# A two-layer decoder trunk: the last layer ends with the tokens on the partitions instead of the channels

## The chip, the cores and the metric

The kernel runs on 1 core of one Trainium2 chip. The metric is the device time of one execution in microseconds (us); lower is better.

## What is computed

256 tokens of 1024 channels (f32) pass through two layers. Each layer has a mixer and then a PEER expert retrieval; the text below is about the end of the second layer's PEER and the final norm:

```python
def block(x_t):                                   # 128 tokens
    ...
    u = u_emb[eidx]; v = v_emb[eidx]              # experts of 128 x 128 product keys
    act = gelu(einsum('thkd,td->thk', u, x_t))
    return einsum('thk,thkd->td', gate * act, v)
...
x = x + g2 * peer(h, ...)                         # g2: one gate per channel, from c
return rmsnorm(x, final_norm)                     # over the 1024 channels of a token
```

The kernel does PEER densely: for each of the 128 first keys it multiplies all tokens with a 1024 x 128 slice of the first table (`u_emb`), keeps gated activations in `ga`/`gb`, and then multiplies these with the slices of the second table (`v_emb`).

## The kernel before, in words

**Layout.** x lies in SBUF as `xt`, 128 partitions of 8 channel chunks x 256 tokens, so that channels are on the partitions: a gate or a norm weight is a scalar per partition, and a sum over channels goes through TensorE with a column of ones.

**Second table, lines 1136 to 1158.** A loop over 126 of the 128 slices. In round i, `csplit(i + 2)` splits one row of the activations into a high part `ch` (ScalarE, L1095) and a rest `cl` (VectorE, L1096). `take()` hands out the slice i and prepares the one two rounds ahead: `hi` on ScalarE (L194), `lo` on VectorE (L201), from `raw`, which SyncE's queue loads from HBM 512 KB at a time (L169), several rounds ahead, each load waiting for a buffer that `lo` frees. Then 12 products of 128x512 (three of hi/lo with ch/cl, for 2 token halves t and 2 channel halves) accumulate in four banks `acc[2 * t + half]` (token rows x 512 channels). Buffers of `ch`, `cl`, `hi` and `lo` are three deep, so the work for round i + 2 waits for the products of round i - 1. The order on each engine is the order in which the code issues.

`xt` is used as scratch during PEER; it is stored to HBM (`x_dram`) before and read back on ScalarE's DMA queue in round 118 (L1148).

**End, lines 1160 to 1221.** The last two slices go bank by bank (6 products each, in the order half, t). Each bank is copied to SBUF (`y`, L1184 to L1187), turned back with 128x128 transposes on TensorE (L1171), multiplied by the gate and added to `xt` (L1175), squared on ScalarE (L367). Squares are added in part on VectorE (L355), and their sum over channels is taken by 1-column products with ones (L377). `rstd` takes root and reciprocal (L384, L385), spreads it over the partitions by a product (L387, L390), and 8 products of x, weight and rstd on VectorE (L1219) give the output, stored in four pieces of 256 KB (L1221) from the queues of SyncE and ScalarE by turns.

Of the kernel before, what the change touches and what calls it, by code (L numbers as in the profile page):

```python
# [10 lines left out]
F32 = mybir.dt.float32  # L11
# [5 lines left out]
AF = mybir.ActivationFunctionType  # L17
OP = mybir.AluOpType
AX = mybir.AxisListType

P = 128
D = 1024
S = 256
NCH = 8
EPS = 1e-6
HEADS = 8
NKEYS = 128
# [10 lines left out]
V_ADAB, V_NMIX, V_NFFN, V_FIN, V_GV, V_PS, V_GS, V_C, NV = 0, 96, 112, 128, 136, 140, 144, 145, 153  # L38
# [8 lines left out]
def trunk(ctx, tc, xT, crow, vecs, consts_in, pos, lamv, bs, cnt, ws, wpool, ada, ev_in, ev_out,  # L47
          od_in, od_out, wq, sk, u_emb, v_emb, out):
    nc = tc.nc
# [7 lines left out]
    dram = ctx.enter_context(tc.tile_pool(name="dram", bufs=1, space=bass.MemoryType.DRAM))  # L57
    ctx.enter_context(tc.manual_schedule())

    dma = nc.sync.dma_start  # L60
# [4 lines left out]
    def aux():  # L65
        return aux_ps.tile([P, 512], F32, name="aux")


    xt = const.tile([P, NCH, S], F32, name="xt")
    vec = const.tile([P, NV], F32, name="vec")  # L70
    cst = const.tile([P, NK], F32, name="cst")
    c_dram = dram.tile([1, D], F32, name="c_dram")
    ident = const.tile([P, P], F32, name="ident")
    iota = const.tile([P, P], F32, name="iota")
    ones = const.tile([P, P], F32, name="ones")
    epst = const.tile([P, 1], F32, name="epst")
# [7 lines left out]
    iotah = const.tile([P, P], F16, name="iotah")  # L84
    nc.vector.tensor_copy(iotah, iota)
    x_dram = dram.tile([P, NCH * S], F32, name="x_dram")
    tabs = const.tile([P, 2, TOPK], F16, name="tabs")
    nc.vector.memset(epst, EPS)
    mod = [const.tile([P, 48], F32, name=f"mod{l}") for l in range(2)]
# [5 lines left out]
    acc = []  # L95
# [48 lines left out]
    def opened(name, **kw):  # L144

        es = ExitStack()
        return es.enter_context(tc.tile_pool(name=name, bufs=1, **kw)), es.close
# [4 lines left out]
    def open_extra(l, n, nr, end):  # L152

        extra["pool"], extra["close"] = right(f"extra{l}")
        extra.update(n=n, raws=nr, most=(n, nr), end=end)
# [54 lines left out]
    def warm():  # L210

        while head["next"] < min(len(stream), head["cap"]) and place(head["next"]):
            if head["issue"]:
                head["issue"]()
                if head["next"] not in units:
                    break
            prep()

    def take():
        k = head["use"]  # L220
        head["use"] = k + 1
        if k < WHOLE:
            if head["issue"]:
                head["issue"]()
            return units[k].rearrange("p (a b) -> p a b", a=NCH), None, k
        warm()
        return (*ready.pop(k), k)

    def free(w):
        if w[2] < WHOLE:  # L230
            del units[w[2]]
            extra["held"].discard(w[2])
        for v in held.values():
            v.discard(w[2])
# [50 lines left out]
    def preload(func):  # L285

        nc.scalar.activation(junk, epst, func)


    def mod_done(l, a, b, src=None):  # L290

        m = a // 12
        bias = vec[:, V_ADAB + 48 * l:V_ADAB + 48 * l + 48]
        if a % 12 < 8:
            c = slice(a - 12 * m, b - 12 * m)
            mv, bv = (v[:, 24 * m:24 * m + 16].rearrange("p (k c) -> p k c", k=2)[:, :, c] for v in (mod[l], bias))
            nc.vector.tensor_add(mv, mv if src is None else src[:, :, None], bv)
            g0 = (V_NMIX, V_NFFN)[m] + 8 * l
            nc.vector.scalar_tensor_tensor(scl[:, l, m, c], mv[:, 1, :], 1.0, vec[:, g0 + c.start:g0 + c.stop],
                                           op0=OP.add, op1=OP.mult)  # L300
        else:
            c = slice(2 * a, 2 * b)
            nc.vector.tensor_add(mod[l][:, c], mod[l][:, c] if src is None else src, bias[:, c])
            if m:
                nc.vector.tensor_scalar(mod[l][:, c], mod[l][:, c], 1.0 / GSCALE, None, op0=OP.mult)
# [6 lines left out]
    def ada_use(l, un, k, r, csil):  # L312

        nc.vector.scalar_tensor_tensor(r, r, 1.0, csil, op0=OP.mult, op1=OP.mult, accum_out=mod_col(l, un, k))

    def ada_job(cols, csil, places):

        nc.gpsimd.dma_start(csil, c_dram.to_broadcast([P, D]))
        order = [(l, un, k, un == b - 1 and k == 1 and a) for l, a, b in cols for un in range(a, b) for k in range(2)]

        def load(n):
            if n < len(order):
                l, un, k, _ = order[n]
                nc.gpsimd.dma_start(places[n % 2], ada[l, un, :, k * D:(k + 1) * D])

        load(0)
        load(1)
        yield 2
        for n, (l, un, k, a) in enumerate(order):
            ada_use(l, un, k, places[n % 2], csil)  # L330
            load(n + 2)
            if a is not False:
                mod_done(l, a, un + 1)
            yield 2
# [498 lines left out]
    def rope_tables(posi, lamt, ang, n):  # L833
# [35 lines left out]
        nc.vector.tensor_scalar(gs, vec[:, V_GS:V_GS + 1], 1.0 - LAM_INIT, None, op0=OP.mult)  # L869
        yield 800  # L870


    def peer(l, acc2, ga):

# [214 lines left out]
        def csplit(i):  # L1089
            if i in csp or i >= NKEYS:  # L1090
                return
            ch = css.tile([P, S], F32R, name="ch", bufs=3)
            cl = css.tile([P, S], F32R, name="cl", bufs=3)
            src = rows(i, 1)[:, 0, :]
            nc.scalar.copy(ch, src)  # L1095
            nc.vector.tensor_tensor(cl, src, ch.bitcast(F32), op=OP.subtract)  # L1096
            csp[i] = (ch, cl)

        def v_mm(i, w, t, half, parts=((0, 0), (1, 0), (0, 1))):

            cs = csp[i]
            for a, b in parts:
                mm(acc[2 * t + half], cs[a][:, t * P:(t + 1) * P],
                   w[b].rearrange("p a b -> p (a b)")[:, half * 512:half * 512 + 512],
                   i == a == b == 0, i == NKEYS - 1 and b == 1)
# [4 lines left out]
        for i in range(NKEYS):  # L1110
# [13 lines left out]
            if i == NKEYS - 3:  # L1124
# [3 lines left out]
                css, cs_close = opened(f"cs{l}")  # L1128
# [4 lines left out]
        if l == 0:  # L1133
            adaw.append(css.tile([P, D], F32, name="adaw"))
            slow.add(ada_job(((0, 20, 24), (1, 0, 8), (1, 8, 12), (1, 12, 20), (1, 20, 24)), csil, adaw))
        for i in range(NKEYS - 2):
            if i == NF + 1:
                gb_close()
                if l == 0:
                    open_extra(1, 3, 2, PRE + 32 + 4)  # L1140
            if i == 72 and l == 0:
                spare = lambda k, n: ga[:, k:k + n, :]
                side.add(rope_tables(spare(0, 1)[:, 0, :].bitcast(I32),
                                     spare(1, 1).rearrange("p a (b c) -> p (a b) c", b=4),
                                     spare(2, 1)[:, 0, :], spare(3, 1)[:, 0, :]))
            if i == NKEYS - 10:
                slow.flush()
                nc.scalar.dma_start(xt.rearrange("p a b -> p (a b)"), x_dram)  # L1148
            csplit(i + 2)
            w = take()  # L1150
            for part in ((0, 0), (1, 0), (0, 1)):
                for t in range(2):
                    for half in range(2):
                        v_mm(i, w, t, half, (part,))
            free(w)
            csp.pop(i)
            side.run(2500)
            slow.run(1)
        side.flush()
        preload(AF.Sqrt)  # L1160
        norm = Norm(lambda c: ga[:, 8 + c, :], ga[:, 16, :], 4)
        ws = [take() for _ in range(2)]
        y = ga[:, 0:8, :].rearrange("p (h t a) b -> p h t (a b)", h=2, t=2)

        def y_turn(half):
# [31 lines left out]
    norm = None  # L1197
    for l in range(2):
        with ExitStack() as es:
            work = es.enter_context(tc.tile_pool(name=f"mix{l}", bufs=1))  # L1200
# [6 lines left out]
        with ExitStack() as es:  # L1207
# [2 lines left out]
            acc2 = [double.tile([P, 2, 512], F32, name=f"acc{k}") for k in range(2)]  # L1210
            acc[:] = [acc2[i // 2][:, i % 2, :] for i in range(4)]
            norm = peer(l, acc2, gpool.tile([P, NKEYS - NF, S], F32, name="ga"))
    with ExitStack() as es:
        work = es.enter_context(tc.tile_pool(name="fin", bufs=1))
        r = norm.rstd(work)
        o = work.tile([P, NCH, S], F32, name="o")
        gains = [vec[:, V_FIN + c:V_FIN + c + 1] for c in range(NCH)]
        for c in range(NCH):
            nc.vector.scalar_tensor_tensor(o[:, c, :], xt[:, c, :], gains[c], r, op0=OP.mult, op1=OP.mult)  # L1219
            if c % 2:  # L1220
                (dma if c % 4 == 1 else nc.scalar.dma_start)(out[:, c - 1:c + 1, :], o[:, c - 1:c + 1, :])  # L1221


def _chunks(v):
# [79 lines left out]
```

## Time and profile before

| | |
|---|---|
| time, median of 3 runs | 1855.11 us (1854.34 to 1855.24) |
| the profiled execution's own time | 1858.97 us |
| its span (first to last instruction) | 1857.3 us |
| TensorE (PE) busy | 1815.0 us, 98% of the span |
| PE's weight loads (PEld) busy | 1648.9 us, 89% |
| VectorE (DVE) busy | 1425.5 us, 77% |
| ScalarE (ACT) busy | 914.4 us, 49% |
| mean granted TensorE clock | 0.986 of full speed |

The busy shares are averages over stages with different limits; the stage that the change touches is the last 100 us. PE overlaps its weight loads with its products. The profiled execution is 3.86 us longer than the median of the others, of which 1.67 us lie outside its span.

### The profile page before, as it was taken

The page shows a single profiled execution, that of the slowest core. Times are in us where ns is not written, and L with a number is a line of the kernel's source. Part 1 is how long each engine was busy: PE and PEld are TensorE (multiplying, and loading weights), DVE is VectorE, ACT ScalarE, POOL GpSimd, SP SyncE. Part 2 cuts the span into 40 slices and gives each one's busy share as a digit, 9 for nine tenths or more (in the row PEclk, how much of TensorE's full clock was granted, in tenths as well). Part 3 has the DMA queues.
Part 4 walks back from the last instruction along what each step waited for, and adds up shares of the span by engine and source line. Part 5 has one row for each costly group of instructions (what it writes and reads, how often), then busy time and mean ns, then how long its engine had stood idle before and what let it go on. Part 6 is the DMA issues. An engine that isn't in the chain of part 4 may idle for free.

```text
span 1857.3 us, 32546 instructions
## 1 busy us (share of the span) xinstructions
PE 1815.0 (98%) x12554; PEld 1648.9 (89%) x12554; DVE 1425.5 (77%) x2994; ACT 914.4 (49%) x1414; POOL 157.6 (8%) x129
## 2 busy tenths in 40 slices
PE   8979999999999999999999899999999999999997
PEld 6769999999998888888788899999999988888886
DVE  6849888888987888887577578978888966666665
ACT  1235555554445554454577455554544455555553
POOL 0007400000000101110000067000000000000000
PEclk9979999999999999999899899999999999999999
DMA  9934555455458898887443345555455556555553
GB/s 386 380 139 157 193 189 169 166 171 172 165 199 271 286 327 290 282 298 256 148 137 118 134 161 196 186 185 170 162 170 169 169 195 193 194 193 192 193 193 124
DMA packets 99616, 375.04 MB, mean 202 GB/s; under 512 B 11330, under 2 KB 11458, under 8 KB 96004
## 3 DMA queue, kind: packets, MB, share of 16 engines
q1 hardware_dynamic: 89714, 335.88, 53.5%
q0 software_dynamic: 8304, 30.15, 4.7%
q10 hardware_dynamic: 1442, 6.92, 1.0%
q8 instruction: 99, 1.62, 0.3%
q14 instruction: 57, 0.47, 0.1%
HBM read 369.76 MB, written 3.15 MB: 201 GB/s over the span
## 4 chain that ended last, share of the span: by engine, by line
PE 89%; DVE 3%; ACT 1%; issue 1%; DVEq 0%; ACTq 0%
PE acc L63 44%; PE mm L63 43%; PE aux L63 1%; DVE lo L201 1%; ACT hi L194 0%; DVE ob L1031 0%; DVE on L772 0%; DVE ga L1049 0%; DVE o L1219 0%; DVE oe L1029 0%; DVE xt L1175 0%; DVE oa L1028 0%; DVE ga L1063 0%; ACT ga L367 0%; ACT mm L1062 0%
## 5 line engine op out<-in xcount | busy, mean ns | idle before, releaser
L63 PE MATMUL mm<-hh,hi 128*128 128x256 f32 x4640 | 817.7, 280 | 0.0
L201 DVE TENSOR_TENSOR lo<-raw,hi 128x1024 fp32r<-128x1024 f32 x526 | 640.9, 1223 | 182.9 <-ACT hi L194 180.5
L63 PEld LDWEIGHTS mm<-hh,hi 128*128 128x128 f32 x4640 | 702.3, 188 | 0.0
L194 ACT CAST hi<-raw 128x1024 fp32r<-128x1024 f32 x576 | 603.4, 1050 | 142.6 <-PE mm L63 83.3
L63 PE MATMUL mm<-hh,lo 128*128 128x256 f32 x2320 | 643.0, 277 | 0.4 <-DVE lo L201 0.4
L63 PEld LDWEIGHTS mm<-hh,lo 128*128 128x128 f32 x2320 | 435.7, 188 | 0.6 <-DVE lo L201 0.6
L63 PE MATMUL acc<-hi,ch 128*128 128x512 f32 x1024 | 277.3, 390 | 0.2 <-DVE ga L1187 0.2
L63 PE MATMUL acc<-lo,ch 128*128 128x512 f32 x1024 | 276.9, 390 | 0.0
L63 PE MATMUL acc<-hi,cl 128*128 128x512 f32 x1024 | 276.9, 390 | 0.0
L63 PEld LDWEIGHTS acc<-hi,ch 128*128 128x128 f32 x1024 | 192.1, 188 | 41.6 <-DVE ga L1187 0.7
L63 PEld LDWEIGHTS acc<-hi,cl 128*128 128x128 f32 x1024 | 192.2, 188 | 41.1
L63 PEld LDWEIGHTS acc<-lo,ch 128*128 128x128 f32 x1024 | 192.2, 188 | 41.1
L1095 ACT CAST ch<-ga 128x256 fp32r<-128x256 f32 x192 | 78.3, 408 | 252.3 <-PE acc L63 252.3
L199 POOL TENSOR_TENSOR lo<-raw,hi 128x1024 fp32r<-128x1024 f32 x50 | 119.6, 2411 | 269.0 <-ACT hi L194 269.0
L1096 DVE TENSOR_TENSOR cl<-ga,ch 128x256 fp32r<-128x256 f32 x192 | 81.4, 424 | 75.1 <-ACT ch L1095 75.1
L1060 ACT ACTIVATE ga<-mm 128x512 f32<-128x512 f32 (+20 forms) x92 | 37.4, 407 | 166.4 <-PE mm L63 166.4
L1031 DVE TENSOR_TENSOR ob<-oe,xt 128x512 f16<-128x512 f16 x256 | 97.5, 422 | 4.4
L63 PE MATMUL acc<-ob,oa 128*128 128x128 f16 x1024 | 80.3, 220 | 0.4
L1063 DVE TENSOR_TENSOR ga<-mm,ga 128x48 f32<-128x48 f32 (+31 forms) x86 | 37.7, 438 | 51.9 <-ACT mm L1062 51.4
L1095 ACT CAST ch<-gb 128x256 fp32r<-128x256 f32 x64 | 25.9, 407 | 77.4 <-PE acc L63 77.4
L63 PEld LDWEIGHTS <-oa 128*128 128x128 f16 x1024 | 57.9, 98 | 5.7 <-issue 0.9
L63 PE MATMUL acc<-hh,hi 128*128 128x256 f32 x224 | 48.1, 317 | 13.0 <-ACT hi L194 9.6
(222 smaller groups left out, 1501.2 us busy)
## 6 DMA issues: line engine op xcount, KB each, us to landing
raw<-in_u_emb_dram SPq DMA_DIRECT2D x256, 512.0 KB, 3.7
raw<-in_v_emb_dram SPq DMA_DIRECT2D x256, 512.0 KB, 4.4
adaw<-in_ada_dram SPq DMA_DIRECT2D x20, 1024.0 KB, 12.6
raw<-in_wq_dram SPq DMA_DIRECT2D x32, 512.0 KB, 5.2
xt<-in_ada_dram POOLq DMA_DIRECT2D x28, 512.0 KB, 7.5
adaw<-in_ada_dram POOLq DMA_DIRECT2D x28, 512.0 KB, 5.1
raw<-in_od_in_dram SPq DMA_DIRECT2D x24, 512.0 KB, 3.4
raw<-in_ev_in_dram SPq DMA_DIRECT2D x12, 512.0 KB, 10.7
```

The source lines that it names most:

```text
L63: nc.tensor.matmul(out_, l, r, start=start, stop=stop, skip_group_check=True)
L194: nc.scalar.copy(hif, r)
L199: nc.gpsimd.tensor_tensor(lof[:, :m], r[:, :m], hif[:, :m].bitcast(F32), op=OP.subtract)
L201: nc.vector.tensor_tensor(lof[:, m:], r[:, m:], hif[:, m:].bitcast(F32), op=OP.subtract)
L1031: nc.vector.tensor_mul(by_two(ob[:, q]), by_two(oe), one(2 + q))
L1060: nc.scalar.activation(v[:, :, t:] if t else v, pair[:, :, t:] if t else pair, AF.Gelu)
L1063: nc.vector.tensor_mul(v[:, :, :t], pair[:, :, :t], v[:, :, :t])
L1095: nc.scalar.copy(ch, src)
L1096: nc.vector.tensor_tensor(cl, src, ch.bitcast(F32), op=OP.subtract)
```

## The change

In the last layer the four banks, which already have tokens on the partitions, are no longer turned back. Instead x is turned in the loop of the second table: in rounds 121 to 124, four transposes each and one copy into `x_td`. The gate and the final norm's weight are needed as rows that lie alike on all partitions: in round 100 each is written as a row to HBM from its columns and read back for all 128 partitions. Scratch is in rows of `ga` whose activations have been used by then. A new function `last` does gate, residual, squares, norm and output. The output's layout changes with it, and the host no longer transposes it. The first layer's end stays as it is.

```diff
+    row_dram = dram.tile([2, D], F32, name="row_dram")
+    def last(ws, v_mm, x_td, z, gbc, nbc, sqs, sums):
+        for t in range(2):
+            for half in range(2):
+                for k in range(2):
+                    v_mm(NKEYS - 2 + k, ws[k], t, half)
+                sl = slice(512 * half, 512 * half + 512)
+                v = z[:, t, sl]
+                nc.vector.tensor_mul(v, acc[2 * t + half], gbc[:, sl])
+                nc.vector.tensor_add(v, v, x_td[:, t, sl])
+                nc.scalar.activation(sqs, v, AF.Square, accum_out=sums[:, 4 * t + half:4 * t + half + 1])
+                nc.vector.tensor_mul(v, v, nbc[:, sl])
+            a, r = sums[:, 4 * t:4 * t + 1], sums[:, 4 * t + 2:4 * t + 3]
+            nc.vector.tensor_add(a, a, sums[:, 4 * t + 1:4 * t + 2])
+            nc.scalar.activation(r, a, AF.Sqrt, bias=epst, scale=1.0 / D)
+            nc.vector.reciprocal(r, r)
+            o = x_td[:, t, :]
+            nc.scalar.activation(o[:, :512], z[:, t, :512], AF.Copy, scale=r)
+            dma(out[:, t, :512], o[:, :512])
+            nc.vector.tensor_scalar(o[:, 512:], z[:, t, 512:], r, None, op0=OP.mult)
+            dma(out[:, t, 512:], o[:, 512:])
+        for w in ws:
+            free(w)
...
+        flat = lambda a, n: ga[:, a:a + n, :].rearrange("p a b -> p (a b)")
+        x_td, z = [flat(a, 8).rearrange("p (t d) -> p t d", t=2) for a in (0, 8)]
+        gbc, nbc, sqs, sums = [flat(a, n) for a, n in ((16, 4), (20, 4), (24, 2), (26, 1))]
         for i in range(NKEYS - 2):
...
+            if l and i == NKEYS - 28:
+                cols = (mod[1][:, 40:48], vec[:, V_FIN:V_FIN + NCH])
+                for k, row in enumerate((gbc, nbc)):
+                    nc.scalar.dma_start(row_dram[k:k + 1, :].rearrange("o (c p) -> p (o c)", p=P), cols[k])
+                    nc.scalar.dma_start(row, row_dram[k:k + 1, :].to_broadcast([P, D]))
+            if l and NKEYS - 7 <= i < NKEYS - 3:
+                t, half = divmod(i - NKEYS + 7, 2)
+                ps = aux()
+                for k in range(4):
+                    nc.tensor.transpose(ps[:, k * P:(k + 1) * P], xt[:, 4 * half + k, t * P:(t + 1) * P], ident)
+                nc.scalar.copy(x_td[:, t, half * 512:half * 512 + 512], ps)
...
+        ws = [take() for _ in range(2)]
+        if l:
+            last(ws, v_mm, x_td, z, gbc, nbc, sqs, sums)
+            cs_close()
+            return None
...
-        r = norm.rstd(work)
-        o = work.tile([P, NCH, S], F32, name="o")
-        gains = [vec[:, V_FIN + c:V_FIN + c + 1] for c in range(NCH)]
-        for c in range(NCH):
-            nc.vector.scalar_tensor_tensor(o[:, c, :], xt[:, c, :], gains[c], r, op0=OP.mult, op1=OP.mult)
-            if c % 2:
-                (dma if c % 4 == 1 else nc.scalar.dma_start)(out[:, c - 1:c + 1, :], o[:, c - 1:c + 1, :])
```

## Rows read from the trace of the kernel before

**Rows 1.** Busy time by stretch: us, PE, PEld, DVE, ACT, POOL, clock, DMA, GB/s

```profile
1800.00:1830.00 30.00, 30.00 (x134) 24.86 (x133) 18.16 (x22) 15.06 (x23) 0.00 (x0) 1.00 0.65 227
1830.00:1858.00 28.00, 17.88 (x93) 14.33 (x91) 14.47 (x29) 8.63 (x18) 0.00 (x0) 0.84 0.10 38
```

**Rows 2.** Timeline of the loop: start, us, engine, line, instructions [idle before <- what ended it]

```profile
1809.47 1.07 PE L63 MATMUL acc<-hi,ch 128*128 128x512 f32 x4
1809.67 0.41 ACT L1095 CAST ch<-ga 128x256 fp32r<-128x256 f32 x1 [1.36 <-PE acc L63]
1809.98 1.05 ACT L194 CAST hi<-raw 128x1024 fp32r<-128x1024 f32 x1
...
1812.19 1.07 PE L63 MATMUL acc<-hi,ch 128*128 128x512 f32 x4
...
1812.47 0.33 ACTq L1148 DMA_DIRECT2D xt<-x_dram  x1
```

**Rows 3.** Timeline of the end, from the last two slices on

```profile
1836.67 0.39 PE L63 MATMUL acc<-hi,ch 128*128 128x512 f32 x1
...
1838.23 0.69 DVE L1187 COPY ga<-acc 128x512 f32<-128x512 f32 x1 [1.46 <-PE acc L63]
...
1840.53 1.02 PEld L1171 LDWEIGHTS mm<-ident,ga 128*128 128x128 f32 x8
...
1848.45 0.26 ACT L384 ACTIVATE rstd<-aux,epst 128x2 f32<-128x2 f32 x1 [0.92 <-PE aux L63]
1848.74 0.17 DVE L385 RECIPROCAL rstd<-rstd 128x2 f32<-128x2 f32 x1 [1.66 <-ACT rstd L384]
...
1850.74 3.22 DVE L1219 SCALAR_TENSOR_TENSOR o<-xt,vec,aux 128x256 f32<-128x256 f32 x8 [1.38 <-PE aux L63]
```

**Rows 4.** Groups of instructions, shapes apart: count | busy us, mean ns | idle before

```profile
L1063 DVE TENSOR_TENSOR ga<-mm,ga 128x512 f32<-128x512 f32 x4 | 2.8, 694 | 5.0 <-ACT mm L1062 5.0
L866 DVE TENSOR_SCALAR rot<-rot,cst 128x256 f32<-128x256 f32 x1 | 0.3, 349 | 0.0
L367 ACT ACTIVATE ga<-xt 128x256 f32<-128x256 f32 x16 | 6.5, 418 | 8.3 <-DVE xt L1175 8.3
L785 ACT ACTIVATE yy<-aux,gs 128x512 fp32r<-128x512 f32 x4 | 2.8, 688 | 4.3 <-PE aux L782 4.3
```

**Rows 5.** Timeline in the second mixer: an activation and the reading of its accumulator

```profile
999.61 0.49 ACT L729 ACTIVATE pr<-acc,mx 128x256 f32<-128x256 f32 x1
999.96 0.22 ACT L729 ACTIVATION_READ_ACCUMULATOR pr<-acc,mx 128x1 f32 x1
```

**Rows 6.** DMA issues of the whole run: KB each, median us from issue to landing

```profile
raw<-in_v_emb_dram SPq DMA_DIRECT2D x256, 512.0 KB, 4.4
x_dram<-xt ACTq DMA_DIRECT2D x2, 1024.0 KB, 4.5
out_dram<-o SPq DMA_DIRECT2D x2, 256.0 KB, 2.1
cst<-in_consts_in_dram ACTq DMA_DIRECT2D x1, 17.0 KB, 5.1
```

**Rows 7.** A queue's waits in the whole run: us in total, times, longest

```profile
SPq L169 <- DVE lo L201: 1011.6, 361, 32.8
```

**Rows 8.** Timeline at the start: ScalarE's queue at a store of a row

```profile
7.06 0.49 ACTq L519 DMA_DIRECT2D c_dram<-csil  x1
7.58 1.28 ACT L287 ACT_TABLE_LOAD   x1 [0.55 <-ACT csil L518]
```

**Rows 9.** Busy time by stretch at the second layer's first norm (columns as Rows 1)

```profile
1048.00:1052.00 4.00, 1.89 (x10) 1.92 (x10) 2.35 (x4) 0.83 (x2) 0.00 (x0) 0.78 0.07 30
1052.00:1056.00 4.00, 1.86 (x6) 1.08 (x5) 1.46 (x4) 0.74 (x3) 0.00 (x0) 0.50 0.00 0
1056.00:1060.00 4.00, 3.92 (x17) 3.69 (x18) 3.94 (x10) 2.48 (x6) 0.00 (x0) 0.50 0.02 4
1060.00:1064.00 4.00, 4.00 (x35) 4.00 (x35) 2.24 (x6) 2.59 (x4) 0.00 (x0) 0.94 0.61 238
```

More of the change, by code (lines that the diff above doesn't have):

```diff
@@ L1160, in peer @@
         preload(AF.Sqrt)
+        ws = [take() for _ in range(2)]
[3 more added lines that the diff above has]
+            return None
         norm = Norm(lambda c: ga[:, 8 + c, :], ga[:, 16, :], 4)
-        ws = [take() for _ in range(2)]
         y = ga[:, 0:8, :].rearrange("p (h t a) b -> p h t (a b)", h=2, t=2)
@@ L1212, in trunk @@
             norm = peer(l, acc2, gpool.tile([P, NKEYS - NF, S], F32, name="ga"))
-    with ExitStack() as es:
-        work = es.enter_context(tc.tile_pool(name="fin", bufs=1))
-        r = norm.rstd(work)
-        o = work.tile([P, NCH, S], F32, name="o")
-        gains = [vec[:, V_FIN + c:V_FIN + c + 1] for c in range(NCH)]
-        for c in range(NCH):
-            nc.vector.scalar_tensor_tensor(o[:, c, :], xt[:, c, :], gains[c], r, op0=OP.mult, op1=OP.mult)
-            if c % 2:
-                (dma if c % 4 == 1 else nc.scalar.dma_start)(out[:, c - 1:c + 1, :], o[:, c - 1:c + 1, :])
 def _chunks(v):
@@ L1297 @@
                                    kind="ExternalInput").ap())
-    args.append(nc.dram_tensor("out_0_dram", (P, NCH, S), F32, kind="ExternalOutput").ap())
+    args.append(nc.dram_tensor("out_0_dram", (P, 2, D), F32, kind="ExternalOutput").ap())
     with tile.TileContext(nc) as tc:
@@ L1302 @@
     got = np.asarray(r.results[0]["out_0_dram"])
-    return np.ascontiguousarray(got.transpose(1, 0, 2).reshape(D, S).T).reshape(1, S, D)
+    return np.ascontiguousarray(got.transpose(1, 0, 2)).reshape(1, S, D)
```

## The prediction

> **What bounds the kernel now.** I read the busy time by stretch first, then the timeline of two rounds of the loop, then the timeline of the end, then the groups for prices, and the DMA views last.
>
> In the loop of the second table TensorE is the bound: busy for 30.00 of 30 us at full clock [rows 1]. One round lasts 2.72 us, from the product at 1809.47 to that at 1812.19 [rows 2]. So whatever TensorE is given there, and whatever makes it wait there, is paid in full. ScalarE has room: ch and hi take about 1.36 us of a round, and it stands idle for another 1.36 us until the products of the round before release its buffers [rows 2]. At the end TensorE falls to 17.88 of 28 us [rows 1]: from the first product of the last two slices (1836.67) to the end of the last VectorE output (1850.74 + 3.22 = 1853.96) it is 17.29 us of copies, turns, squares and products that wait on each other [rows 3]. The change works on these 17.29 us, pays with work inside the loop, and adds four DMAs on ScalarE's queue.
>
> **The transposes of x.** 16 transposes enter TensorE's full loop. Eight of the old kind take 1.02 us [rows 3], so sixteen cost 2.04 us, with nothing to hide them. The four copies to `x_td` (about 0.6 us on ScalarE, a 512-wide activation in [rows 4] being 0.69) fall in rounds 121 to 124. There the preparation of hi is 3.9 us early: it ends 1.56 us into a round (1809.98 + 1.05 = 1811.03 against 1809.47) and is used two rounds, 5.44 us, after that round began [rows 2]. A copy with its wait for the transposes, some 1.2 us, fits: 0. x is read back at 1812.47, and round 121 begins about 10.6 us later; a 1 MB store took 4.5 us [rows 6], so I count no wait for it.
>
> **The new end.** Its first bank is ready 1.56 us after the first product, as before (1838.23 against 1836.67) [rows 3]. Per bank:
> - gate product from PSUM 0.69 on VectorE [rows 4], the addition of the same size the same, and 0.03 from one step to a dependent one (1848.45 + 0.26 to 1848.74) [rows 3];
> - the square on ScalarE: 0.42 for 256 wide [rows 4]; a copy of 1024 takes 1.05 [rows 2], so 0.21 for each further 256, and I estimate 0.63 for 512; reading the accumulator ends 0.08 after the activation (999.96 + 0.22 against 999.61 + 0.49) [rows 5];
> - the weight product 0.69. It overwrites the very tile that the square reads, so VectorE must stand still during the square; the next bank's products are queued behind it.
>
> With handovers of 0.02 to 0.03 this is 2.86 us for a bank, 2.78 where the next instruction is independent and overlaps by 0.08. TensorE needs 1.36 us for a bank's six products (half a round), so it is never late again. After two banks (5.64) come the 1-wide addition 0.10, root 0.26 and reciprocal 0.17 with their handovers 0.50 (those of the old norm, [rows 3]), and the last scaling. VectorE's half: between 0.35 (256 wide) and twice that, 0.70 [rows 4], I take the middle, 0.52; ScalarE's half, at most 0.69 [rows 4], I take 0.65. Tokens 0 to 127 free VectorE after 6.71 us, and tokens 128 to 255 end at 6.71 + 5.64 + 0.60 + 0.03 + 0.65 = 13.6 us. From the first product: 1.56 + 13.6 = 15.2 us against 17.29, a gain of 2.1 us. It is almost exactly what the transposes in the loop cost: together 0.0 us (-0.05).
>
> **The stores.** Before, the last of four 256 KB stores was alone behind the last product. Now two become ready within 0.15 us on one queue. Stores of this kind move 0.26 MB in about 0.8 us (four pieces follow the four pairs of VectorE products, 8 in 3.22 us [rows 3], and each still lands in 2.1 us [rows 6]). The second lands about one such piece later: +0.8 us. Bounds: 0 if they overlap fully, +1.0.
>
> **The rows of gate and weight.** This is the large term. In round 100 ScalarE's queue gets: store 1 (a row out of columns), load 1 (that row for all partitions), store 2, load 2. Load 1 reads what store 1 wrote, and load 2 what store 2 wrote, so each load must wait until its store has landed, and it waits in ScalarE's queue. That a DMA instruction holds its queue is seen twice: SyncE's queue stood 1011.6 us for its buffers [rows 7], and ScalarE's table load began only when the issue of a store before it was over (7.06 + 0.49, 7.58) [rows 8]. Behind the waiting loads stand ch(102) and hi(102), and TensorE waits for them.
>
> How much may the queue stand? The issue comes right after a round's hi has been handed to the engine, 0.28 us into the round before (1812.47 against 1812.19, for the issue of round 118) [rows 2]. hi(102) must be ready three rounds after the start of round 99, 8.16 us. After release, ch and hi need 1.4 us. The queue may stand 8.16 - 1.4 - 0.28 = 6.5 us.
>
> How long does it stand?
> - Store 1: no row of before stores single floats. From below 2.1 us (a store of 256 KB on quiet queues), from above 5.1 us (a load in 128 small pieces of 136 B beside a full stream) [rows 6]. I take the middle, 3.6.
> - Issue of load 1: 0.33 [rows 2].
> - Store 2 stands in the DMA queue behind load 1, 512 KB, as large as a slice, whose median is 4.4 us [rows 6]. From below 4.4, from above 4.4 + 5.1 = 9.5; I take 4.4 + 2.1 = 6.5, one quiet store after one load. If it does not queue behind the load at all, 2.1.
> - Issue of load 2: 0.33.
>
> Sum: 3.6 + 0.33 + 6.5 + 0.33 = 10.8 us, and TensorE waits 10.8 - 6.5 = 4.3 us. Bounds: 7.2 - 6.5 = 0.7 and 15.3 - 6.5 = 8.8; without queueing behind the load 4.9, below 6.5, so 0. What comes after a late hi(102) recovers: ch and hi need 1.4 us of each 2.72.
>
> A rule that speaks against the change: the Trainium skill, DMA: Bandwidth & Descriptors, Rules for kernel authors, says that a transfer with a strided last dimension becomes one descriptor per element; here 1,024 per store, 64 for each of the 16 engines. No row of before shows such a store. By it I would go to the upper ends: 9.6 us more in all, 1864.7.
>
> A wait of several us may also cost clock. Around 1050 TensorE was busy for less than half of 8 us, the granted clock fell to 0.50 (1.2 GHz), and after it was busy again (3.92 of 4 us) it stayed at 0.50 until 1060, to be 0.94 after [rows 9]. Half speed for about 4.2 us loses 2.1 us. I leave it out of the sum and give it to a rival, because these rows show a stretch of little work and not one gap.
>
> **Sum.** Transposes +2.0, new end -2.1, stores +0.8, wait for the rows +4.3: +5.1 us. Against the profiled execution: span 1857.3 + 5.1 = 1862.4, its own time 1858.97 + 5.1 = 1864.1. The median of the runs is 3.86 us below that execution; 1855.11 + 5.1 = 1860.2 us.
>
> **Rivals.**
> 1. *The rows fit into the slack* (not slower). Place: round 100; it decides from a stand of 6.5 us downward. For it: the low ends, 2.1 us for a store, and store 2 not held up by load 1. Against: a slice's load alone takes 4.4 us beside the stream. Time: 1855.11 + 0.8 = 1855.9. The Trainium skill, same page, Anatomy of one DMA, gives about 2.0 us plus bytes at 436 GB/s for each DMA (fitted on GpSimd's queue); by it the queue would stand about 2.0 + 0.33 + 1.2 + 2.0 + 0.33 = 5.9 us (an estimate), and this rival would hold. The loads here take 4.4 us where it gives 3.2.
> 2. *A long stand, with the clock.* 8.8 + 2.1 + 0.8 = +11.7: 1866.8. For it: small pieces, and the half-speed stretch in [rows 9]. Against: only 1,024 floats per store.
> 3. *A clearly shorter end.* If VectorE need not wait for the square (0.74 with its handover, four times), the end is 3.0 us shorter, and with no stand and no late store the time is 1852.1. Against: the same tile is read and overwritten. Even that is within 0.2%; faster needs cheaper transposes too.
>
> **How the numbers follow.** 0.2% is 3.7 us, about what a measurement of this kernel can tell from no change. Chances: forecast (a wait of 0.7 to 6 us at full clock) 0.45; rival 1 0.28; rival 2 0.20; rival 3 0.07. Slower by over 0.2% needs a wait above 2.9 us: about three quarters of the forecast (0.34) and rival 2, 0.54. Same: the rest of the forecast, rival 1, and 0.02 of rival 3, 0.41. Faster: 0.05. The range reaches from rival 1 with an end 0.9 us shorter (1855.0) nearly to rival 2 (1866.0); the forecast's own range is 1856.6 to 1861.9.
>
> **What would show it.** Right: in the timeline of round 100 two loads on ScalarE's queue several us apart, ScalarE idle, then a gap on TensorE ended by hi; the transposes as 0.5 us in each of rounds 121 to 124; VectorE waiting 0.7 us for each square; from the first product of the last slices to the last scaling about 15.2 us; two stores at the end. Wrong: no gap on TensorE in rounds 100 to 104 (rival 1), a granted clock of 0.5 there (rival 2), or banks that take about 2.1 us (rival 3).

## The result and the profile after

| | before | after |
|---|---|---|
| time, median | 1855.11 us (1854.34 to 1855.81, 5 runs) | 1874.10 us (1871.55 to 1877.24, 5 runs) |
| ratio | | 1.0099 [1.0084, 1.0114] |
| profiled execution, own time | 1858.97 us | 1872.98 us |
| its span | 1857.3 us | 1871.3 us |
| first product of the second layer's last loop | 1493.91 us | 1490.24 us |
| from there to the end of the span | 363.4 us | 381.1 us |

The change makes the kernel about 1% slower: +19.0 us between the medians, where +5.1 was forecast. The last two rows of the table are the better yardstick for the parts. The loop begins at different times in different executions (1485.40 to 1494.26 us over all profiles of this study), and that scatter, which between these two kernels lies ahead of everything changed, drops out. From the loop's start to the end the change costs 17.7 us.

First the timeline of the rounds around the rows' DMAs; before, each round there was like the two in [rows 2].

```profile
1759.81 0.38 ACTq L1177 DMA_DIRECT2D row_dram<-mod  x1
...
1766.79 1.07 PE L63 MATMUL acc<-lo,ch 128*128 128x512 f32 x4
1770.66 0.34 ACTq L1178 DMA_DIRECT2D ga<-row_dram  x1
1771.03 0.46 ACTq L1177 DMA_DIRECT2D row_dram<-vec  x1
1780.85 0.33 ACTq L1178 DMA_DIRECT2D ga<-row_dram  x1
1781.27 0.40 ACT L1120 CAST ch<-ga 128x256 fp32r<-128x256 f32 x1 [20.18 <-DMA row_dram<-vec]
...
1782.68 2.07 PE L63 MATMUL acc<-hi,ch 128*128 128x512 f32 x4 [14.82 <-ACT hi L195]
...
1787.57 1.09 PE L63 MATMUL acc<-hi,ch 128*128 128x512 f32 x4
```

The queue holds as predicted, but far longer. Store 1 is issued at 1759.81 and load 1 only at 1770.66; store 2 at 1771.03 and load 2 at 1780.85. With the end of load 2's issue (1781.18) the queue has stood for 21.4 us. ScalarE's next work, ch(102), starts at 1781.27, and TensorE waits for hi for 14.82 us. The round after the gap takes 4.89 us (1782.68 to 1787.57) instead of 2.72.

The chain of waits leads through the same four DMAs:

```profile
1759.81 10.83 DMA row_dram<-mod
1770.66 0.34 ACTq L1178
...
1771.03 9.80 DMA row_dram<-vec
1780.85 0.33 ACTq L1178
...
1782.68 54.06 PE acc L63 x228
```

Before, TensorE was busy throughout the loop [rows 1]; now the chain leaves it for 23 us. The busy time by stretch shows the clock (columns as in [rows 1]):

```profile
1768.00:1772.00 4.00, 0.00 (x0) 0.00 (x0) 0.00 (x0) 0.00 (x0) 0.00 (x0) 0.75 0.31 17
1772.00:1784.00 12.00, 1.32 (x3) 1.13 (x4) 1.77 (x3) 2.73 (x5) 0.00 (x0) 0.50 0.21 52
1784.00:1788.00 4.00, 4.00 (x12) 3.09 (x12) 2.83 (x4) 1.36 (x3) 0.00 (x0) 0.61 0.94 316
1788.00:1792.00 4.00, 4.00 (x19) 3.27 (x18) 2.15 (x4) 2.49 (x4) 0.00 (x0) 1.00 0.60 196
```

All engines stand still from 1768 to 1772. The granted clock falls to 0.50, the level of 1.2 GHz, and is still there for most of the first round after the gap (0.61 on average from 1784 to 1788): that round loses 2.2 us. It is what [rows 9] showed, here after a single gap.

Next the end, in the timeline: turning x, the first bank, and the tokens' last scaling. It answers to [rows 3].

```profile
1836.57 0.60 PE L1183 MATMUL aux<-ident,xt 128*128 128x128 f32 x4
...
1852.05 0.39 PE L63 MATMUL acc<-hi,ch 128*128 128x512 f32 x1
...
1853.61 0.69 DVE L881 TENSOR_TENSOR ga<-acc,ga 128x512 f32<-128x512 f32 x1 [1.46 <-PE acc L63]
...
1854.36 0.50 PE L63 MATMUL acc<-hi,ch 128*128 128x512 f32 x1 [0.79 <-DVE ga L881]
...
1855.06 0.63 ACT L883 ACTIVATE ga<-ga 128x512 f32<-128x512 f32 x1 [2.66 <-DVE ga L882]
...
1855.82 0.69 DVE L884 TENSOR_TENSOR ga<-ga 128x512 f32<-128x512 f32 x1 [0.79 <-ACT ga L883]
...
1866.86 0.72 ACT L890 ACTIVATE ga<-ga 128x512 f32<-128x512 f32 x1 [0.23 <-DVE ga L888]
```

From the first product (1852.05) to the end of the last scaling (1867.58) it is 15.5 us against 17.29. The square takes the estimated 0.63 us and VectorE waits for it (0.79 to 0.85 idle, four times). One wait was not foreseen: TensorE waits for VectorE's first gate product, since the banks of both channel halves of a token half lie in one tile; it cost nothing here, because VectorE sets the pace.

### The profile page after: what moved, and what is told of

It is laid out like the page before. It is cut to its first block, busy times and chain, and to the rows that moved or that the text cites. A ratio compares the mean times of both kernels' runs of the same rounds, so it can differ in the third digit from the quotient of the medians.

```text
span 1871.3 us, 32501 instructions
## 1 busy us (share of the span) xinstructions
PE 1811.1 (97%) x12532; PEld 1643.1 (88%) x12532; DVE 1424.5 (76%) x2988; ACT 915.6 (49%) x1419; POOL 157.4 (8%) x129
## 4 chain that ended last, share of the span: by engine, by line
PE 87%; DVE 3%; DMA 2%; ACT 1%; issue 1%; ACTq 0%; SPq 0%; DVEq 0%
PE acc L63 43%; PE mm L63 43%; PE aux L63 1%; DVE lo L202 1%; DMA row_dram<-mod 1%; DMA row_dram<-vec 1%; ACT hi L195 0%; DMA raw<-in_v_emb_dram 0%; DVE ob L1056 0%; DVE on L773 0%; DVE ga L1074 0%; ACT ga L883 0%; DVE ga L882 0%; DVE ga L884 0%; DVE oe L1054 0%
## 5 line engine op out<-in xcount | busy, mean ns | idle before, releaser
L63 PE MATMUL acc<-hi,ch 128*128 128x512 f32 x1024 | 278.9, 392 | 19.6 <-ACT hi L195 14.8
L63 PEld LDWEIGHTS acc<-hi,ch 128*128 128x128 f32 x1024 | 192.2, 188 | 62.0 <-ACT hi L195 15.2
```

The lines of the kernel that those rows point to most:

```text
L63: nc.tensor.matmul(out_, l, r, start=start, stop=stop, skip_group_check=True)
```

## The experiments

Two theories were told apart first. **Theory Q:** the loads hold ScalarE's queue until their stores have landed, and the stores take long. **Rival S:** the DMAs starve the stream of slices. Later experiments ask what makes the stores slow and what the rest of the change is worth. In the diffs, lines are shortened to what differs. The kernel before ran beside them: 1856.31 us (17 runs) for the first four, 1856.28 us (29 runs) for the next four, 1857.94 us (one run) for the ninth.

**1. Both stores early.** They go where the second layer's mixer begins; the loads stay in round 100.

```diff
-                    nc.scalar.dma_start(row_dram[k:k + 1, :].rearrange("o (c p) -> p (o c)", p=P), cols[k])   # round 100
+                for k in range(2):                                                                            # mixer
+                    nc.scalar.dma_start(row_dram[k:k + 1, :].rearrange("o (c p) -> p (o c)", p=P), cols[k])
```

> The two stores of single floats are issued at the start of the second layer's mixer, some 850 us earlier; the two loads stay in round 100 on ScalarE's queue and find the rows landed. Theory Q (ScalarE's queue stands for the landings, and hi of round 102 comes late): the gap of 14.8 us on TensorE and the 2.1 us at half clock go, 1874.1 - 16.9 = about 1857; ScalarE's queue stands under 1 us in round 100. Rival S (the single floats hold the DMA engines, so that the slices' loads come late wherever the stores are): the gap moves into the mixer, where slices stream as well, and the time stays above 1865.

1858.33 us (10 runs), ratio 1.0014 [1.0003, 1.0024]. The loads follow each other at once, in the timeline of round 100:

```profile
1757.40 0.33 ACTq L1176 DMA_DIRECT2D ga<-row_dram  x1
1757.75 0.46 ACTq L1176 DMA_DIRECT2D ga<-row_dram  x1
```

No product of the loop waits. From the loop's start to the end it is 363.9 us, 0.5 above before. Theory Q holds: the same bytes on the same queue cost nothing once no load waits for its store. The stores, issued back to back with no load between them, still took 10.5 and 10.2 us. They met no stream there: from 911 to 924 us no slice is loaded. So they are slow by themselves, and what they do to a stream this experiment does not show.

**2. All four on GpSimd's queue**, written in round 100.

```diff
+                    nc.gpsimd.dma_start(row_dram[k:k + 1, :].rearrange("o (c p) -> p (o c)", p=P), cols[k])
+                    nc.gpsimd.dma_start(row, row_dram[k:k + 1, :].to_broadcast([P, D]))
```

> All four DMAs stay in round 100 but go on GpSimd's queue, which has nothing behind it. Theory Q: nobody waits for that queue, so about 1857 as with early stores. Rival S: each store still holds the slices' loads for about 6 us; two of them are more than the 8.5 us by which the loads run ahead, so a gap of 3 us or more on TensorE remains, now ended by a load: 1860 or more.

1860.57 us (8 runs), ratio 1.0023 [1.0012, 1.0035]. The DMAs did not stay in round 100. GpSimd's queue had no other work left and ran ahead of the loop, as far as data and scratch were ready; in the timeline:

```profile
1148.51 0.95 POOL L1177 DMA_DIRECT2D row_dram<-mod  x1
...
1161.88 1.05 ACT L195 CAST hi<-raw 128x1024 fp32r<-128x1024 f32 x1 [4.64 <-DMA raw<-in_u_emb_dram]
...
1164.24 0.38 PE L63 MATMUL mm<-hh,lo 128*128 128x256 f32 x1 [0.46 <-DVE lo L202]
...
1629.49 0.91 POOL L1177 DMA_DIRECT2D row_dram<-vec  x1
```

Store 1 (12.1 us) went out in the loop of the first table. Store 2 (9.8 us) went out around round 49 of the last loop, with load 1 just ahead of it (1628.95) and load 2 after its landing (1639.82). The last loop pays nothing for them: TensorE is busy for 10.00 of 10 us from 1620 to 1670, and from the loop's start to the end it is 364.4 us. That is theory Q: only who is queued behind the wait matters there.

But rival S is not empty. Beside store 1 the loads of slices come late: hi waits 6.6 us for them in three waits, and TensorE 1.4 us in three, where none of the other kernels waits for a load. These 1.4 us lie ahead of the last loop, and would be a part of the 2.2 us by which the median stands above the first experiment's; by the number set for it (1860 or more) rival S would have won. It does not explain the gap of 14.8 us: there ScalarE waits for its own queue (20.18 us, ended by store 2), not for a slice.

**3. One row only**: the gate's row, and the weight product reads it too.

```diff
-                for k, row in enumerate((gbc, nbc)):
+                nc.scalar.dma_start(row_dram[0:1, :].rearrange("o (c p) -> p (o c)", p=P), mod[1][:, 40:48])
+                nc.scalar.dma_start(gbc, row_dram[0:1, :].to_broadcast([P, D]))
```

> Only the gate's row is stored and loaded in round 100 on ScalarE's queue; the norm weight's row is left out (the weight product takes the gate's row instead). Theory Q: the queue stands 10.8 + 0.4 = 11.2 us instead of 21.4, and TensorE's gap is 11.2 - 6.5 = 4.7 us instead of 14.8; span about 10 to 12 us below that of the changed kernel. Rival S: one store delays the loads by about 6 us, less than the 8.5 us by which they run ahead: no gap at all.

1866.18 us in one run. In its timeline, the queue and TensorE:

```profile
1763.11 0.38 ACTq L1175 DMA_DIRECT2D row_dram<-mod  x1
1774.19 0.34 ACTq L1176 DMA_DIRECT2D ga<-row_dram  x1
1774.62 0.40 ACT L1120 CAST ch<-ga 128x256 fp32r<-128x256 f32 x1 [10.24 <-DMA row_dram<-mod]
1776.03 1.88 PE L63 MATMUL acc<-hi,ch 128*128 128x512 f32 x4 [4.88 <-ACT hi L195]
...
1780.47 1.07 PE L63 MATMUL acc<-hi,ch 128*128 128x512 f32 x4
```

One row makes the queue stand 11.4 us (1763.11 to the end of the load's issue, 1774.53) and TensorE wait 4.88: the allowance of 6.5 us again. Even this shorter gap costs clock (0.57 from 1776 to 1780): the round after it took 4.44 us, 1.7 more. From the loop's start to the end it is 371.0 us, 10.1 below after.

**4. What makes the store slow.** To the first experiment's kernel six more stores of 4 KB or less are added in rounds 62 to 92, each read back on GpSimd's queue, where nobody waits. The read back starts some 0.5 us after the store has landed (4.5 in the view of DMA issues for the one that reads 5.0 here).

```diff
+                dst = d.rearrange("o (c p) -> p (o c)", p=P)                      # neighbours: n floats
+                dst = d.rearrange("o (c p s) -> p (o c) s", p=P, s=16)[:, :, 0]   # 64 B apart
+                dst = d.rearrange("o (p c) -> p (o c)", p=P)                      # 128 pieces of 32 B
+                dst, src = d.rearrange("o (c p) -> c (o p)", p=P), ident[0:8, :]  # 8 pieces of 512 B
+                nc.scalar.dma_start(dst, src)
+                nc.gpsimd.dma_start(ga[0:1, 27, 0:back.shape[1]], back)
```

> Early stores as before, and six extra stores in rounds 62 to 92, one every six rounds on ScalarE's queue, each read back on GpSimd's queue so that its landing is seen; nothing else waits for them. If each single float written costs its own time at the memory: 1,024 floats about 10 us, 512 about 6.5, 256 about 4.5, 1,024 floats 64 B apart again about 10, 128 pieces of 32 B about 3, 8 pieces of 512 B about 2.5. If neighbours from different DMA engines in one line are the cost: the floats 64 B apart land in under 5 us. If it is a fixed latency beside the stream: all six about 10 us.

**9. The distance of the floats.** The same with other stores (run last, shown here because it continues the fourth): 1,024 floats 8 to 128 B apart, and 128 neighbours.

```diff
+                dst = d.rearrange("o (c p s) -> p (o c) s", p=P, s=w)[:, :, 0]    # w = 2, 4, 8, 16, 32 floats
+                dst, src = d.rearrange("o p -> p o"), src[:, :1]                  # 128 neighbours
```

> The kernel with the two stores issued early, and six more stores of single floats in rounds 62 to 92 of the last loop, each from ScalarE's queue and read back on GpSimd's queue, where nobody waits behind them: 1,024 floats 8, 16, 32, 64 and 128 B apart, and 128 neighbouring floats, one from each partition. If what costs is that neighbours lie in one line of 64 B, the landing times fall with the distance in the first three: between the 11.8 us of neighbours (4 B apart) and the 4.4 us of 64 B apart, which comes again, and 128 B apart lands in 4.4 us or a little less; the 128 neighbours, 8 lines with 16 writers each, land in 8 to 9.5 us like the 256 and 512 before. If what costs is a line of 32 B, 32 B apart lands in 4.4 us already. If what costs is a larger block (512 B, or a page of the memory), 64 B apart was only a step on the way and 128 B apart lands clearly sooner than 4.4 us, towards the 2.7 us of whole lines. The time of the kernel as a whole says nothing here (a few us around the first experiment's).

Issues and read backs of the fourth experiment, in its timeline:

```profile
1656.06 0.38 ACTq L1189 DMA_DIRECT2D p<-vec  x1
1668.48 0.52 POOL L1191 DMA_DIRECT2D ga<-p  x1 [520.06 <-DMA p<-vec]
...
1707.14 0.37 ACTq L1189 DMA_DIRECT2D pwide<-vec  x1
1712.07 0.48 POOL L1191 DMA_DIRECT2D ga<-pwide  x1 [11.18 <-DMA pwide<-vec]
...
1738.06 0.30 ACTq L1189 DMA_DIRECT2D pline<-ident  x1
1741.31 0.48 POOL L1191 DMA_DIRECT2D ga<-pline  x1 [14.08 <-DMA pline<-ident]
```

and two pairs of the ninth:

```profile
1655.97 0.38 ACTq L1186 DMA_DIRECT2D w<-vec  x1
1662.85 0.52 POOL L1187 DMA_DIRECT2D ga<-w  x1 [514.84 <-DMA w<-vec]
...
1737.57 0.34 ACTq L1186 DMA_DIRECT2D p<-vec  x1
1747.58 0.48 POOL L1187 DMA_DIRECT2D ga<-p  x1 [20.32 <-DMA p<-vec]
```

Each store's time is the second start minus the first (the kernels' own times, 1855.95 and 1855.50 us in one run each, matter no further), with one measurement for each entry:

| store | us from issue to read back |
|---|---|
| neighbouring floats (4 B apart): 1,024, 512, 256, 128 | 12.4, 9.6, 10.2, 10.0 |
| 1,024 floats 8 B apart | 6.9 |
| 16, 32, 64, 128 B apart | 5.9, 5.1, 4.9 and 5.9, 5.5 |
| 128 pieces of 32 B | 5.0 |
| 8 pieces of 512 B | 3.3 |

Not the number of pieces: 128 floats are almost as slow as 1,024, and 1,024 floats apart are twice as fast. What costs is that single floats from different partitions lie right beside each other. The unit stays open. The fall with the distance and the slow 128 neighbours fit lines of 64 B, but most of the cost is gone at 8 B already, and from 16 B on the differences are no larger than those between the two runs of 64 B. No product of the loop waits beside these twelve stores, and from the loop's start to the end it is 364.4 and 364.0 us (363.9 in the first experiment): in the last loop rival S costs half a microsecond at most.

The Trainium skill, DMA: Bandwidth & Descriptors, Specifications, says that pieces under 512 B are written by reading, modifying and writing back. The runs agree that 512 B pieces land soonest; that neighbours cost twice what floats apart cost the Trainium skill does not say there, and no run shows what happens inside.

**5. The weight product into a tile of its own** (first experiment's kernel), so that VectorE need not wait for the square.

```diff
-                nc.vector.tensor_mul(v, v, nbc[:, sl])
+                nc.vector.tensor_mul(zw[:, t, sl], v, nbc[:, sl])
```

> Early stores, and the weight product writes to a tile of its own, so that VectorE need not wait for the square. Theory (VectorE's stand for each square sets the length of the new end): a bank takes 2.05 us instead of 2.86, and the end from the first product of the last slices to the last scaling is 12.5 us instead of 15.5: about 3 us below the kernel with early stores. Rival (TensorE or ScalarE is as late): under 1 us of it shows.

1855.12 us (10 runs), ratio 0.9995 [0.9984, 1.0007]. In the timeline the square and the weight product start together, and a new wait follows:

```profile
1839.95 0.63 ACT L883 ACTIVATE ga<-ga 128x512 f32<-128x512 f32 x1 [2.66 <-DVE ga L882]
1839.95 0.69 DVE L884 TENSOR_TENSOR ga<-ga 128x512 f32<-128x512 f32 x1
...
1840.96 0.69 DVE L881 TENSOR_TENSOR ga<-acc,ga 128x512 f32<-128x512 f32 x1 [0.31 <-PE acc L63]
```

The end takes 13.6 us, 2.0 less than after; 3.0 were expected. Of the rest 0.6 us went into VectorE's wait for TensorE (0.31, twice), which had itself been held by the two banks of one tile. The other 0.4 is where the sum for a token half still waits for the square of its second bank.

**6. The DMAs alone**: the kernel before with the four DMAs added in round 100; the rows are not used.

```diff
+            if l and i == NKEYS - 28:
+                for k in range(2):
+                    nc.scalar.dma_start(row_dram[k:k + 1, :].rearrange("o (c p) -> p (o c)", p=P), cols[k])
+                    nc.scalar.dma_start(row, row_dram[k:k + 1, :].to_broadcast([P, D]))
```

> The kernel before, with nothing but the four DMAs of the two rows added in round 100 on ScalarE's queue; the rows go into scratch that nothing reads, so the output is the old one. Theory Q: the whole loss comes with them, a gap of about 15 us on TensorE in rounds 102 to 103 and 2 us at half clock, 17 us over the kernel before. Rival (the new end and the transposes carry a part of the loss): under 12 us.

1873.04 us in one run; from the loop's start to the end 380.2 us, 16.8 above before. Its TensorE after the gap:

```profile
1781.78 2.07 PE L63 MATMUL acc<-hi,ch 128*128 128x512 f32 x4 [14.60 <-ACT hi L195]
```

The DMAs alone cost 16.8 of the 17.7 us.

**7. The rows stored in lines**: TensorE turns the columns in round 90, and each row leaves in 8 pieces of 512 B. Place and queue are those of after.

```diff
-                    nc.scalar.dma_start(row_dram[k:k + 1, :].rearrange("o (c p) -> p (o c)", p=P), cols[k])
+                    nc.scalar.dma_start(row_dram[k:k + 1, :].rearrange("o (c p) -> c (o p)", p=P), turned[0:8, 0, k * P:(k + 1) * P])
```

> The changed kernel, but TensorE turns the two sets of columns in round 90, so that each row is stored in 8 pieces of 512 B; place and queue of the DMAs as in the changed kernel. If the single floats are the price: each store lands in about 3 us (2.7 in the run with store shapes), the second behind its load in about 6, the queue stands 9 us in place of 21.4, and TensorE's gap is about 2.5 us: 1858 to 1861. If any store and load in turn would stand so long: the gap stays above 10 us.

1857.19 us (10 runs), ratio 1.0012 [0.9997, 1.0026]. The queue in its timeline:

```profile
1755.22 0.30 ACTq L1176 DMA_DIRECT2D row_dram<-ga  x1
1757.99 0.33 ACTq L1177 DMA_DIRECT2D ga<-row_dram  x1
1758.35 0.35 ACTq L1176 DMA_DIRECT2D row_dram<-ga  x1
1762.98 0.33 ACTq L1177 DMA_DIRECT2D ga<-row_dram  x1
1764.80 1.20 PE L63 MATMUL acc<-hi,ch 128*128 128x512 f32 x4 [1.54 <-ACT hi L195]
...
1767.68 1.07 PE L63 MATMUL acc<-hi,ch 128*128 128x512 f32 x4
```

The same waits at the same place, with stores of 2.8 and 4.6 us: the queue stands 8.1 us, TensorE waits 1.54 (8.1 - 6.5 = 1.6), and the clock is kept (1.00 from 1764 to 1768; the round after takes 2.88). How long the stores take is the cause of the size of the loss. Store 2, behind load 1, took 1.9 us longer than store 1; in this one trace, queueing behind the load is worth that at most.

**8. A shorter end** (first experiment's kernel): banks in the order in which their tiles come free, x turned straight into PSUM (its second token half during the end), rstd and weight in one step of VectorE, one weight product on GpSimd.

```diff
+            nc.vector.scalar_tensor_tensor(o[:, t, sl(half)], z[:, t, sl(half)], one(4 * t + 2), nbc[:, sl(half)],
+                                           op0=OP.mult, op1=OP.mult)
...
+        nc.gpsimd.tensor_tensor(zw, z[:, 1, :512], nbc[:, :512], op=OP.mult)
...
+                mm(acc[2 * half + t if l else 2 * t + half], cs[a][:, t * P:(t + 1) * P],
```

> Early stores, and an end that keeps VectorE busy: banks in the order of the two-bank tiles, x turned straight into PSUM (the second token half during the end), rstd and weight in one product, one weight product on GpSimd. Worked out from the durations of the changed kernel: 10.1 us from the first product of the last slices to the last scaling in place of 15.5, and 0.9 us less of transposes in the loop: about 6 us below the kernel with early stores, 4 below the kernel before. If the end is bound by something else than VectorE's waits, it is no faster than the kernel before.

1850.69 us (12 runs), ratio 0.9973 [0.9960, 0.9986]: faster than both kernels, by 0.3% against before. TensorE no longer waits for VectorE. From the first product to the last scaling, in its timeline, it is 10.17 us (1843.11 - 1832.94):

```profile
1832.94 0.39 PE L63 MATMUL acc<-hi,ch 128*128 128x512 f32 x1
...
1842.39 0.72 ACT L921 ACTIVATE ga<-ga 128x512 f32<-128x512 f32 x1 [0.50 <-DVE ga L920]
```

## Why the prediction was right in its mechanism and wrong in its size

The failed step is the term "store 1 3.6, store 2 6.5" in the stand of the queue. The argument went from the nearest rows, 2.1 to 5.1 us, and took 5.1 as an upper bound; but [rows 6] hold no store of single floats, and pieces of 136 B do not bound pieces of 4 B that lie side by side. Measured:

| term | predicted | measured |
|---|---|---|
| store 1, issue to load 1's issue | 3.6 (bounds 2.1 to 5.1) | 10.8 |
| store 2, issue to load 2's issue | 6.5 (bounds 4.4 to 9.5) | 9.8 |
| the queue stands | 10.8 | 21.4 |
| allowance before TensorE waits | 6.5 | 6.6 (21.4 - 14.8) |
| TensorE's wait | 4.3 | 14.8 |
| clock after it | 0 (2.1 in rival 2) | 2.2 |
| transposes in rounds 121 to 124 | 2.0 | 1.9 (3.19 - 2.72 = 0.47, four times) |
| new end | 15.2 | 15.5 (-1.8 against before) |
| late stores | +0.8 | +0.4 (3.7 us from last scaling to end of span; before 3.3) |

The measured terms give 14.8 + 2.2 + 1.9 - 1.8 + 0.4 = 17.5 us, against 17.7 from the loop's start to the end. So the place, the holding of the queue and the allowance were right, and experiments 1, 3, 6 and 7 show each by itself. The wait's size alone is 10.5 us of the miss, the clock 2.2 more.

**Store 2's reason was wrong too.** It was priced as queueing behind load 1. Experiment 1 has no load between the stores, and the second took 10.2 us all the same; in experiment 7, where stores are short, the queueing is worth 1.9 us at most.

**Rival 1** fell: the stand was three times the slack. The Trainium skill, DMA: Bandwidth & Descriptors, Anatomy of one DMA, gave 5.9 us for it; the trace does not agree, with 21.4 us. The Trainium skill's rule on that page against strided last dimensions spoke in the right direction, but names no price for a store, and the upper ends that I would have gone to by it (9.6 us more in all) were short as well. Its count of one piece per element is not the price either: 1,024 floats 64 B apart landed in 4.9 and 5.9 us.

**Rival 2** had the mechanism that came, the stand with the clock behind it; with a stand of at most 15.3 us it was 7.3 us short of the median. I had kept the clock out of the sum because [rows 9] did not show a single gap; gaps of 4.9 and 14.8 us both cost it (1.7 and 2.2 us), one of 1.5 us didn't.

**Rival 3** was right to look at VectorE's wait for the square: experiment 5 frees it and gains 2.0 us at the end. With that the change is even (0.9995), and it takes experiment 8's rebuilt end to make it pay.

## What to carry to other kernels

Before a DMA that depends on another is put on a compute engine's queue, list what is queued behind it and take the time from the first issue to the last landing off that work's slack; here moving two stores some 850 us ahead (to 912 us) took back nearly all of the loss. Another queue takes the wait off the engine, but a DMA on an idle queue goes as soon as its data is there, not at the place where the code stands (experiment 2). Don't price a store by its bytes or by the nearest row when its pieces are much smaller than any in the trace: turn columns into rows on chip first (two transposes, 0.25 us) and store whole lines. When a new last stage is bounded by an engine that waits for others, look for a tile that is read and overwritten, and for two banks in one tile.

## What the runs showed of the hardware that was not expected

The pieces of such a store leave quickly and land late. The DMA view counts packets where they start (packets, MB, share of 16 engines' time that these packets take in all). In after, store 1's queue is q10; from 1762.5 to 1763.5 us:

```profile
q10 hardware_dynamic: 917, 0.00, 51.6%
```

With 123 in the microsecond before, these are all of store 1's 1,040 packets, but it lands at 1770.6. While such a store is landing, the packets of the slices take longer. Experiment 2 shows it best, because there the loads of slices go on; their queue, q1, beside store 1, from 1151 to 1152 and from 1153 to 1154:

```profile
q1 hardware_dynamic: 79, 0.26, 76.2%
...
q1 hardware_dynamic: 21, 0.09, 134.5%
```

A packet of a slice takes 0.15 us (76.2% of 16 us for 79) as the store goes out, and 1.0 us (134.5% of 16 us for 21) two microseconds later; one load of a slice takes 11.8 us there, where 3.7 is the median. That points to a wait behind the DMA engines, where the writes arrive, with other traffic caught in it; no run shows it directly. Where the slices are loaded far enough ahead no product waits, as in the last loop (experiments 4 and 9, and store 2 of experiment 2); in the loop of the first table it cost TensorE 1.4 us.
